# Hybrid decoder trunk: a linear recurrence in chunks of 64 tokens instead of 32

## The chip, the cores and the metric

One core of one Trainium2 chip runs the whole program. The metric is the device time of one execution in microseconds, lower is better. All matrix work is on TensorE (PE in the rows; its weight loads are PEld); VectorE (DVE), ScalarE (ACT) and GpSimd (POOL) do the elementwise work; SyncE (SP) issues the large loads.

## What is computed

Two layers on 256 tokens of width 2048. Each: a modulated RMS norm, one projection `h @ W_in`, four groups of heads side by side (A: an RWKV-7 recurrence, B: stick-breaking attention, C: dilated attention, D: differential attention), `concat @ W_out`, a residual, a second norm and a SwiGLU block. The change is in A, eight heads of width 64:

```python
def step(state, inp):
    r_t, w_t, k_t, v_t, kk_t, b_t = inp
    sa = jnp.einsum('bhvk,bhk->bhv', state, -kk_t)
    state = (state * w_t[:, :, None, :] + sa[..., None] * b_t[:, :, None, :]
             + v_t[..., None] * k_t[:, :, None, :])
    return state, jnp.einsum('bhvk,bhk->bhv', state, r_t)
...
mu = jnp.mean(y, axis=-1, keepdims=True)
y = ((y - mu) * lax.rsqrt(var + RWKV_LN_EPS)).reshape(B, S, C) * ln_w + ln_b
return (y + bonus.reshape(B, S, C)) * g
```

In layer 1, `v` is first mixed with the `v` of layer 0.

## The kernel before

The weights stream in through SyncE's queue; ScalarE and VectorE split most of them into a high and a low float32r part (tiles `hi`, `lo`), and TensorE takes three products for each (names `hh`, `hl` for the activations). The order of all instructions is written at build time by a small planner: `quad` (line 534) writes the weight products, and between them `tick` (484) lets generators ("jobs") write their next piece once their inputs should be ready by an estimated clock (`spend`, 250). Each engine then runs its instructions in that order. PSUM has four banks for jobs, handed out by `bank` (309) and `drop` (320). `rwkv` (942) runs at a higher priority than the attention jobs; `self.width` bounds how many of these run at once.

Group A goes in three stages. (1) `rw_head_pair` (828), for two heads at a time: decays, scaled keys, `kq` (removal keys and receptances), then lines 892 to 907: products of the keys with `kq` for each chunk of 32 tokens, in a bank for each head of the pair, masked by VectorE into `ab`; `bh`, `kh` and `v` are transposed into `TM`. (2) `rwkv` lines 995 to 1024: the 64 triangular 32x32 blocks are inverted by substitution on VectorE (tiles `at`, `xt`, `iv`), through DRAM (`scr`, `scr2`) into `TT`. (3) Lines 1026 to 1104: eight steps, one for each chunk. `state_part` and `chunk_part` are the products of state and of values; a step has three hand-overs (`yield`): sums for the keys, evacuated by ScalarE to `sa0`; the inverse, evacuated to `sa`; the new state, evacuated by VectorE to `S`, and the sums for the outputs, which stay in two banks `XY` for four steps. `group_norm` (1123) then normalises four chunks at a time, adds `bonus` and multiplies by `gate` (both kept in SBUF since stage 1). The projection `W_out` reads the tiles `ys` in the order B and C, A, D (`WO`, line 30) and the build waits for a tile that isn't written yet (`need`, 528).

In the rows a product in plain float32 shows as two MATMUL instructions. All lines of the trace carry L180, the helper that records each operation, so groups are told apart by their tiles: `m<-S,kq` is state by keys, `m<-tm,ab` values by key products, `m<-sa,TT` the inverse, `m<-tm` and `m<-sa,tm` the new state, `m<-sa,ab` the corrected values for the outputs, `m<-kq,a` and `m<-kq,sh` the key products of a head pair, `q<-...` weight products, `m<-qk,qk` scores, `m<-v,aT` a product of group D.

## Time and profile before

| | |
|---|---|
| median of three runs | 2662.35 us (2657.1 to 2662.5) |
| the profiled execution | 2661.86 us, span 2660.1 us, mean granted clock 0.986 |
| TensorE busy | 2594.6 us (98% of the span) |
| VectorE, ScalarE, GpSimd busy | 1802.8, 1121.6, 107.6 us |

A row of the timeline has the start in microseconds from the span's beginning, the time from the first start to the last end of the group, the engine, the tiles written and read, rows*columns of the array and the shape of the moving operand, and the count; in brackets the idle time of the engine before it and what ended it. Matmuls overlap, so the time that a group takes from TensorE is the distance between its start and that of the next row. The rows of a stretch give the busy time of each engine in it, then the granted TensorE clock (1.00 is 2.4 GHz, 0.50 is 1.2 GHz), the mean busy share of the DMA engines and GB/s.

### The profile page before, as it was taken

How to read it: one execution, taken by the hardware profiler on the slowest of the kernel's cores; microseconds unless marked ns; L12 is line 12 of the kernel's file. 1: busy time of each engine (PE TensorE's matmuls, PEld its weight loads, DVE VectorE, ACT ScalarE, POOL GpSimd, SP SyncE). 2: the span in 40 equal slices, each digit the busy share in tenths (PEclk: the TensorE clock that was granted, in tenths of full speed). 3: DMA queues.
4: the chain of work that ended last, by engine and by line, in shares of the span. 5: the costliest groups of instructions: out<-in, count | busy, mean ns of one | idle time of the engine just before them, and what ended most of it. 6: DMA issues, size and time to landing. Idle time of an engine off the chain costs nothing.

```text
span 2660.1 us, 43002 instructions
## 1 busy us (share of the span) xinstructions
PE 2594.6 (98%) x17446; PEld 2296.8 (86%) x17446; DVE 1802.8 (68%) x2922; ACT 1121.6 (42%) x1579; POOL 107.6 (4%) x208
## 2 busy tenths in 40 slices
PE   7999999999999999999999999999999999999998
PEld 4888887887898898898899998889888988988987
DVE  6667875669887787764577888677755455455555
ACT  2315543324434433433455444456444344344343
POOL 0001110000000000000020011000100000000001
PEclk9999998999999999999999999999899999999999
DMA  9895664897888898865466677576455555555553
GB/s 357 310 373 205 228 221 164 280 347 267 322 338 324 315 340 316 308 230 190 175 256 255 252 281 253 209 254 247 147 186 190 190 188 182 185 189 190 186 188 117
DMA packets 133609, 648.70 MB, mean 244 GB/s; under 512 B 17685, under 2 KB 23853, under 8 KB 86177
## 3 DMA queue, kind: packets, MB, share of 16 engines
q1 hardware_dynamic: 126306, 632.66, 65.0%
q0 software_dynamic: 6528, 12.25, 1.5%
q8 instruction: 136, 2.23, 0.3%
q10 hardware_dynamic: 576, 1.05, 0.1%
q14 instruction: 63, 0.52, 0.1%
HBM read 640.61 MB, written 7.62 MB: 244 GB/s over the span
## 4 chain that ended last, share of the span: by engine, by line
PE 90%; DVE 4%; DMA 3%; ACT 1%; issue 1%; SPq 0%; DVEq 0%; ACTq 0%
PE q L180 75%; PE m L180 14%; DMA ar<-wada 2%; DVE ar L180 1%; DVE lo L180 1%; DVE x L180 0%; PE st L180 0%; DMA raw<-wst 0%; DMA x<-xt 0%; ACT hi L180 0%; DVE rstd L180 0%; DVE out L180 0%; ACT sh L180 0%; SPq L180 0%; ACT L180 0%
## 5 line engine op out<-in xcount | busy, mean ns | idle before, releaser
L180 DVE TENSOR_TENSOR lo<-raw,hi 128x1024 fp32r<-128x1024 f32 (+1 forms) x742 | 903.1, 1225 | 531.1 <-ACT hi L180 526.1
L180 ACT ACTIVATE hi<-raw 128x1024 fp32r<-128x1024 f32 (+1 forms) x742 | 779.8, 1057 | 936.8 <-PE q L180 756.4
L180 DVE SCALAR_TENSOR_TENSOR ar<-ar,cond 128x1024 f32<-128x1024 f32 x384 | 462.6, 1219 | 42.3 <-DMA ar<-wada 41.6
L180 PE MATMUL q<-hi,hh 128*128 128x512 f32 x1456 | 457.0, 395 | 6.8 <-ACT hh L180 6.8
L180 PE MATMUL q<-lo,hh 128*128 128x512 f32 x1456 | 455.6, 394 | 0.0
L180 PE MATMUL q<-hi,hl 128*128 128x512 f32 x1456 | 451.9, 392 | 0.0
L180 PEld LDWEIGHTS q<-hi,hh 128*128 128x128 f32 x1456 | 271.7, 190 | 63.2 <-ACT hh L180 7.9
L180 PEld LDWEIGHTS q<-hi,hl 128*128 128x128 f32 x1456 | 275.0, 189 | 58.7
L180 PEld LDWEIGHTS q<-lo,hh 128*128 128x128 f32 x1456 | 272.4, 189 | 58.2 <-issue 1.7
L180 PE MATMUL q<-ah,hi 128*128 128x256 f32 x1344 | 216.6, 283 | 0.0
L180 PE MATMUL q<-ah,lo 128*128 128x256 f32 x1344 | 216.1, 283 | 0.0
L180 PE MATMUL q<-al,hi 128*128 128x256 f32 x1344 | 216.1, 283 | 0.0
L180 PEld LDWEIGHTS q<-ah,hi 128*128 128x128 f32 x1344 | 185.9, 192 | 0.6
L180 PEld LDWEIGHTS q<-al,hi 128*128 128x128 f32 x1344 | 185.5, 192 | 0.0
L180 PEld LDWEIGHTS q<-ah,lo 128*128 128x128 f32 x1344 | 185.5, 192 | 0.0
L180 PE MATMUL q<-hh,hi 128*128 128x256 f32 (+1 forms) x1040 | 179.6, 293 | 5.1 <-ACT hh L180 3.4
L180 PE MATMUL q<-hh,lo 128*128 128x256 f32 (+1 forms) x1040 | 178.7, 292 | 4.2 <-DVE lo L180 4.1
L180 PE MATMUL q<-hl,hi 128*128 128x256 f32 (+1 forms) x1040 | 172.6, 286 | 0.0
L180 PEld LDWEIGHTS q<-hh,hi 128*128 128x128 f32 (+1 forms) x1040 | 148.2, 195 | 12.4 <-issue 4.9
L180 PEld LDWEIGHTS q<-hh,lo 128*128 128x128 f32 (+1 forms) x1040 | 146.9, 195 | 10.7 <-DVE lo L180 5.3
L180 PEld LDWEIGHTS q<-hl,hi 128*128 128x128 f32 (+1 forms) x1040 | 146.2, 194 | 0.1
L180 POOL TENSOR_TENSOR sq<-sq,sq 128x256 f32<-128x256 f32 x44 | 35.1, 798 | 1684.0 <-ACT sq L180 1681.5
(243 smaller groups left out, 2496.3 us busy)
## 6 DMA issues: line engine op xcount, KB each, us to landing
raw<-wst SPq DMA_DIRECT2D x369, 1024.0 KB, 4.9
ar<-wada SPq DMA_DIRECT2D x384, 512.0 KB, 6.7
whole<-wst SPq DMA_DIRECT2D x64, 512.0 KB, 7.5
x<-xt SPq DMA_DIRECT2D x32, 128.0 KB, 4.5
bias<-bskew POOLq DMA_DIRECT2D x24, 128.0 KB, 3.6
bskew<-bscr POOLq DMA_DIRECT2D x4, 576.0 KB, 14.0
xd<-x POOLq DMA_DIRECT2D x16, 128.0 KB, 6.9
x<-xd SPq DMA_DIRECT2D x16, 128.0 KB, 3.9
```

The costliest lines, as they stand in the source:

```text
L180: return f(*a, **kw)
```

## The change

The recurrence runs in four chunks of 64 tokens. `kq` holds, for each chunk, 64 columns of removal keys and 64 of receptances, the order turned round in odd chunks. The products of values for the keys and for the outputs share one weight tile `kar` of 128 columns, so one product writes the sums for the outputs to one half of the partitions and those for the keys to the other. The state is kept block-diagonal for two heads (128x128 in `Sx`, zero elsewhere), so state by keys and by receptances is one product for a head pair. The inverse of a 64x64 triangle is put together from two 32x32 inverses (by the same substitution) and a product of both with the block below the diagonal (tiles `NT`, `XT`, `XN`, `VS`, `TQ`). The outputs of each chunk are centred on their own and one bank is held for a chunk instead of two for four chunks. `bonus`, `gate` and the first layer's `v` go to DRAM and are loaded back where they are used. The pool of 128x512 tiles has 21 slots instead of 19, and the width for group D is 2 instead of 3. The core of the diff:

```diff
-    jj, t = p[:, None] % 32, np.arange(32)[None, :]
+    jj, t = p[:, None] % 64, np.arange(64)[None, :]
...
-    put("msk", np.concatenate([-strict, incl, strict, incl], 1))
-    put("seg", np.broadcast_to((np.arange(264) % 33 != 0).astype(np.float32), (128, 264)))
+    low = p[:, None] < 64
+    put("msk", np.concatenate([-strict, incl, np.where(low, incl, strict), np.where(low, strict, incl)], 1))
+    put("seg", np.broadcast_to((np.arange(264) % 65 != 0).astype(np.float32), (128, 264)))
...
     def T2(self, dt=F32, n="d"):
-        return self.heap.tile([128, 512], dt, tag="k2", name=self.name(n), bufs=self.cfg.get("k2", 19))
+        return self.heap.tile([128, 512], dt, tag="k2", name=self.name(n), bufs=self.cfg.get("k2", 21))
 
...
         kqj = self.T2(n="kq")
-        kq4 = kqj[:].rearrange("p (c s t) -> p c s t", s=2, t=32)
-        tt(kq4[:, :, 1, :], c3(r[j][:]), e23[:, :, 1:33], ALU.mult)
+        kq3 = kqj[:]
+        kq_r, kq_a = (bass.AP(tensor=kq3.tensor, offset=kq3.offset + o, ap=[list(kq3.ap[0]), [256, 2], [st, 2], [1, 64]])
+                      for o, st in ((0, 192), (64, 64)))
+        c4 = lambda ap: ap.rearrange("p (h g) t -> p h g t", g=2)
+        tt(kq_r, c4(c3(r[j][:])), c4(e23[:, :, 1:65]), ALU.mult)
...
+        if l == 0:
+            nc.gpsimd.dma_start(self.vfirst[j], v[j][:])
         bn = self.T(n="bn")
         tt(bn[:], p3[:, 0:256], v[j][:], ALU.mult)
         self.drop()
-        R["bonus"][j] = bn
-        yield
-        dbc = dall[:, j, :, None].to_broadcast([128, 8, 32])
+        nc.gpsimd.dma_start(R["gb"][j, :, 0, :], bn[:])
+        R["bonus"][j] = True
...
         ab = yield from self.bank(2)
-        absb = self.T2(n="ab")
-        ab3 = absb[:].rearrange("p (q n) -> p q n", q=4)
-        for e in range(2):
-            es = slice(64 * e, 64 * e + 64)
-            for c in range(8):
-                g, hf = c % 4, c // 4
-                for s, m in enumerate((bt, kt)):
-                    o = hf * 128 + s * 64
-                    nc.tensor.matmul(ab[e][32 * g:32 * g + 32, o:o + 64], m[es, c * 32:c * 32 + 32],
-                                     kq4[es, c, :, :], start=True, stop=True)
-        for e in range(2):
-            tt(ab3[:, 2 * e:2 * e + 2, :], ab[e][:, 0:256].rearrange("p (q n) -> p q n", q=2),
-               C("msk")[:, None, :].to_broadcast([128, 2, 128]), ALU.mult)
+        ba, br, kar = self.T(n="ba"), self.T(n="br"), self.T2(n="kar")
+        ba4, br4, kar4 = (t[:].rearrange("p (e h n) -> p e h n", e=2, h=2) for t in (ba, br, kar))
+        for s, m in enumerate((bt, kt)):
+            for hf in range(2):
+                for g in range(2):
+                    c = 2 * hf + g
+                    ks = [(0, 0, 128)] if s or g else [(0, 64, 64), (64, 0, 64)]
+                    for o, i, n in ks:
+                        for e in range(2):
+                            es = slice(64 * e, 64 * e + 64)
+                            o1 = hf * 256 + s * 128 + o
+                            nc.tensor.matmul(ab[e][64 * g:64 * g + 64, o1:o1 + n], m[es, c * 64:c * 64 + 64],
+                                             kqj[es, c * 128 + i:c * 128 + i + n], start=True, stop=True)
+        for t4, o, n in ((ba4, 0, 64), (br4, 64, 64), (kar4, 128, 128)):
+            for e in range(2):
+                tt(t4[:, e, :, :], ab[e].rearrange("p (h n) -> p h n", h=2)[:, :, o:o + n],
+                   C("msk")[:, None, o:o + n].to_broadcast([128, 2, n]), ALU.mult)
         self.drop(2)
-        nc.gpsimd.dma_start(R["scr"][4 * j:4 * j + 4].rearrange("q p t -> p q t"), ab3[:, :, 0:32])
+        nc.gpsimd.dma_start(R["scr"][4 * j:4 * j + 4].rearrange("q p t -> p q t"),
+                            ba[:].rearrange("p (q n) -> p q n", q=4))
...
+        R["AB"][j] = (br4, kar4)
...
-            d = self.vfirst[j]
+            d = self.T(n="vf")
+            nc.gpsimd.dma_start(d[:], self.vfirst[j])
...
+        sc_ = scr[:]
+        for e in range(2):
             for i in range(2):
-                nc.gpsimd.dma_start(at[i][64 * e:64 * e + 64, :], sc3[:, 512 * i:512 * i + 512])
+                for b in range(2):
+                    nc.gpsimd.dma_start(at[i][64 * e + b:64 * e + 64:2, :],
+                                        bass.AP(tensor=sc_.tensor, offset=sc_.offset + b * 2080 + i * 1024,
+                                                ap=[[4096, 32], [64, 16], [1, 32]]))
...
-        TTt = self.T2(n="TT")
-        TT3 = TTt[:].rearrange("p (q t) -> p q t", t=32)
+        NT = self.T2(n="NT")
+        for a in range(2):
+            nc.gpsimd.dma_start(NT[64 - 64 * a:128 - 64 * a, :].rearrange("p (q t) -> p q t", t=32),
+                                scr[:, 64 * a:64 * a + 64, 32:64].rearrange("q p t -> p q t"))
+        TQ = [self.T2(n="TT") for _ in range(2)]
+        for t in TQ:
+            nc.gpsimd.memset(t[:], 0.0)
+        XT, XN, VS = self.T2(n="XT"), self.T2(n="XN"), self.T2(n="VS")
+        X3, N3, XN3, V3 = (t[:].rearrange("p (q t) -> p q t", t=32) for t in (XT, NT, XN, VS))
         s2 = scr2[:]
         for e in range(2):
-            nc.gpsimd.dma_start(TT3[e:128:2], bass.AP(tensor=s2.tensor, offset=s2.offset + e * 64 * 512,
-                                                      ap=[[32, 64], [2048, 16], [1, 32]]))
-        yield
-
...
+                                            ap=[[32, 32], [2048, 16], [1, 32]]))
+        yield
+
+        T4 = [t[:].rearrange("p (q t) -> p q t", t=64) for t in TQ]
+        nc.vector.transpose(XN[:], XT[:])
+        for i in range(2):
+            for g in range(4):
+                P = slice(32 * g, 32 * g + 32)
+                o = g % 2 * 32
+                nc.scalar.activation(T4[i][P, :, o:o + 32], X3[P, 8 * i:8 * i + 8, :], AF.Copy)
+        yield
+        vp = yield from self.bank()
+        for q in range(16):
+            for a in range(2):
+                P, N = slice(64 * a, 64 * a + 32), slice(64 * a + 32, 64 * a + 64)
+                nc.tensor.matmul(vp[N, q * 32:q * 32 + 32], N3[P, q, :], XN3[P, q, :], start=True, stop=True)
+        for a in range(2):
+            N = slice(64 * a + 32, 64 * a + 64)
+            nc.scalar.activation(VS[N, :], vp[N, :], AF.Copy)
+        self.drop()
...
+        vp = yield from self.bank()
+        for q in range(16):
+            for a in range(2):
+                P, N = slice(64 * a, 64 * a + 32), slice(64 * a + 32, 64 * a + 64)
+                nc.tensor.matmul(vp[P, q * 32:q * 32 + 32], V3[N, q, :], X3[N, q, :], start=True, stop=True)
+        v3 = vp[:].rearrange("p (q t) -> p q t", t=32)
+        for a in range(2):
+            P = slice(64 * a, 64 * a + 32)
+            for i in range(2):
+                nc.scalar.activation(T4[i][P, :, 32:64], v3[P, 8 * i:8 * i + 8, :], AF.Copy)
+        self.drop()
+        yield
...
+        Sx = self.T2(n="S")
+        nc.gpsimd.memset(Sx[:], 0.0)
+        for c in range(4):
+            g, hf = c % 2, c // 2
+            P, H = slice(64 * g, 64 * g + 64), slice(64 - 64 * g, 128 - 64 * g)
             if g == 0:
-                XY = yield from self.bank(2)
                 sa0, sa = self.T2(n="sa0"), self.T2(n="sa")
-
-            def state_part(col, which, Sx):
+                yc, mu = self.T2(n="yc"), self.small(8)
+            vc = TM[hf][P, 2, :]
+            XY = yield from self.bank()
+            for h in range(8):
+                j, e = divmod(h, 2)
+                nc.tensor.matmul(XY[:, h * 64:h * 64 + 64], AB[j][1][P, e, hf, :], vc[:, h * 64:h * 64 + 64],
+                                 start=h == 0, stop=c == 0, skip_group_check=True)
+            if c:
                 for j in range(4):
-                    for e in range(2):
-                        es = slice(64 * e, 64 * e + 64)
-                        nc.tensor.matmul(XY[e][P, col + j * 64:col + j * 64 + 64], kq[j][es, c, which, :],
-                                         Sx[es, j * 64:j * 64 + 64], start=j == 0, stop=False, skip_group_check=True)
-
-            def chunk_part(col, w, rhs, st, en):
+                    nc.tensor.matmul(XY[:, j * 128:j * 128 + 128], kq[j][:, c * 128:c * 128 + 128],
+                                     Sx[:, j * 128:j * 128 + 128], start=False, stop=True, skip_group_check=True)
+            nc.scalar.activation(sa0[H, :], XY[H, :], AF.Copy, scale=-1.0)
...
-            if c:
-                state_part(0, 0, Sx)
-            chunk_part(0, 64, TM[hf][P, 2, :], c == 0, True)
-            s3 = sa0[P, :].rearrange("p (j e v) -> p j e v", j=4, e=2)
-            for e in range(2):
-                o3 = XY[e][P, 0:256].rearrange("p (j v) -> p j v", j=4)
-                if e and self.cfg.get("sd", 0):
-                    nc.vector.tensor_scalar(s3[:, :, e, :], o3, -1.0, None, ALU.mult)
-                else:
-                    nc.scalar.activation(s3[:, :, e, :], o3, AF.Copy, scale=-1.0)
...
             p1 = yield from self.bank()
             for h in range(8):
-                nc.tensor.matmul(p1[P, h * 64:h * 64 + 64], TT3[P, 2 * h + hf, :], sa0[P, h * 64:h * 64 + 64],
-                                 start=True, stop=True)
+                nc.tensor.matmul(p1[P, h * 64:h * 64 + 64], T4[h // 4][H, 2 * (h % 4) + hf, :],
+                                 sa0[H, h * 64:h * 64 + 64], start=True, stop=True)
             nc.scalar.activation(sa[P, :], p1[P, :], AF.Copy)
             self.drop()
             yield
-            Sprev = Sx
-            if c < 7:
+            if c < 3:
                 p2 = yield from self.bank()
-                for s, m in ((1, TM[hf][P, 2, :]), (0, sa[P, :])):
+                for s, m in ((1, vc), (0, sa[P, :])):
                     for h in range(8):
                         j, e = divmod(h, 2)
                         es = slice(64 * e, 64 * e + 64)
                         nc.tensor.matmul(p2[es, j * 64:j * 64 + 64], TM[hf][P, s, h * 64:h * 64 + 64],
                                          m[:, h * 64:h * 64 + 64], start=s == 1 and j == 0, stop=s == 0,
                                          skip_group_check=True)
-                Sx = self.T(n="S")
...
+                for e in range(2):
+                    es = slice(64 * e, 64 * e + 64)
+                    d3 = Sx[es, :].rearrange("p (j v) -> p j v", j=4)[:, :, 64 * e:64 * e + 64]
+                    p3 = p2[es, 0:256].rearrange("p (j v) -> p j v", j=4)
+                    if Sd is None:
+                        nc.vector.tensor_copy(d3, p3)
+                    else:
+                        tt(d3, p3, Sd[es, :].rearrange("p (j v) -> p j v", j=4), ALU.add)
...
-            if c:
-                state_part(256, 1, Sprev)
-            chunk_part(256, 96, TM[hf][P, 2, :], c == 0, False)
-            chunk_part(256, 32, sa[P, :], False, True)
-            if g == 3:
-
-                mu, var = self.small(8), self.small(8)
...
-                self.add(self.group_norm(l, hf, yc, sq, var, R), 1)
+            for h in range(8):
+                j, e = divmod(h, 2)
+                nc.tensor.matmul(XY[P, h * 64:h * 64 + 64], AB[j][0][P, e, hf, :], sa[P, h * 64:h * 64 + 64],
+                                 start=False, stop=True, skip_group_check=True)
+            yield
...
+            y3 = XY[P, :].rearrange("p (h v) -> p h v", h=8)
+            nc.vector.tensor_reduce(mu[P, :], y3, mybir.AxisListType.X, ALU.add)
+            nc.vector.tensor_scalar(mu[P, :], mu[P, :], -1.0 / 64, None, ALU.mult)
+            tt(yc[P, :].rearrange("p (h v) -> p h v", h=8), y3, mu[P, :, None].to_broadcast([64, 8, 64]), ALU.add)
+            self.drop()
+            if g == 1:
+                self.add(self.group_norm(l, hf, yc, self.T2(n="ysq"), self.small(8), R), 1)
...
-            R["gate", j] = g
+            nc.gpsimd.dma_start(R["gb"][j, :, 1, :], g[:])
+            R["gate", j] = True
...
+        gb = []
+        for j in range(4):
+            t = self.T(n="gb")[:].rearrange("p (w n) -> p w n", w=2)
+            nc.gpsimd.dma_start(t, R["gb"][j, :, :, hs])
+            gb.append(t)
...
             yo = R["yo"][j]
-            nc.vector.tensor_tensor(yo[:, hs], yo[:, hs], R["bonus"][j][:, hs], ALU.add)
-            nc.vector.tensor_tensor(yo[:, hs], yo[:, hs], R["gate", j][:, hs], ALU.mult)
+            nc.vector.tensor_tensor(yo[:, hs], yo[:, hs], gb[j][:, 0, :], ALU.add)
+            nc.vector.tensor_tensor(yo[:, hs], yo[:, hs], gb[j][:, 1, :], ALU.mult)
...
-                    self.width = self.cfg.get("dw", 3)
+                    self.width = self.cfg.get("dw", 2)
```

## Rows read from the trace of the kernel before

**Rows 1.** The page: totals of TensorE, and the chain that ended last by engine.
```profile
PE 2594.6 (98%) x17446; PEld 2296.8 (86%) x17446; DVE 1802.8 (68%) x2922; ACT 1121.6 (42%) x1579; POOL 107.6 (4%) x208
PE 90%; DVE 4%; DMA 3%; ACT 1%; issue 1%; SPq 0%; DVEq 0%; ACTq 0%
```

**Rows 2.** Stretches: busy time (instructions) of each engine, clock, DMA share, GB/s.
```profile
378.20:494.70 116.50, 114.74 (x1292) 96.19 (x1292) 59.63 (x157) 40.38 (x92) 4.32 (x8) 0.91 0.59 198
1490.00:1625.00 135.00, 133.97 (x1198) 123.99 (x1196) 120.91 (x234) 60.54 (x89) 16.54 (x37) 1.00 0.74 264
1625.00:1747.50 122.50, 122.10 (x1441) 106.63 (x1440) 79.70 (x160) 54.50 (x103) 7.93 (x20) 0.96 0.62 217
```

**Rows 3.** Timeline of TensorE through one step of the recurrence in layer 0.
```profile
443.97 1.07 PE L180 MATMUL m<-tm,ab 32*32 32x64 f32 x16
444.98 0.73 PE L180 MATMUL q<-lo,hh 128*128 128x512 f32 x2
...
449.65 1.08 PE L180 MATMUL m<-sa,TT 32*32 32x64 f32 x16
...
452.92 0.68 PE L180 MATMUL m<-tm 32*64 32x64 f32 x16 [0.61 <-ACT aT L180]
453.43 0.64 PE L180 MATMUL m<-sa,tm 32*64 32x64 f32 x16
454.00 0.64 PE L180 MATMUL m<-S,kq 64*32 64x64 f32 x16
454.56 1.08 PE L180 MATMUL m<-tm,ab 32*32 32x64 f32 x16
455.48 1.05 PE L180 MATMUL m<-sa,ab 32*32 32x64 f32 x16
456.46 0.55 PE L180 MATMUL m<-consts,e 128*128 128x128 f32 x3
```

**Rows 4.** Timeline of TensorE: key products of a head pair, 64 instructions in all.
```profile
293.89 0.34 PE L180 MATMUL m<-kq,a 64*32 64x64 f32 x8
...
294.96 0.87 PE L180 MATMUL m<-aT,v 128*64 128x256 f32 x8
```

**Rows 5.** Timeline of TensorE: products of 128x128 with 128 moving columns.
```profile
525.60 1.50 PE L180 MATMUL m<-v,aT 128*128 128x128 f32 x12
526.94 0.60 PE L180 MATMUL q<-yo,whole 128*128 128x256 f32 x2
```

**Rows 6.** Groups by shape: weight loads of 128 and 32 columns (busy us, mean ns).
```profile
L180 PEld LDWEIGHTS m<-v,aT 128*128 128x128 f32 x48 | 6.2, 192 | 0.2
L180 PEld LDWEIGHTS m<-sa,TT 32*32 32x32 f32 x256 | 14.6, 105 | 3.9 <-issue 1.0 <-ACT sa L180 0.6 <-ACT aT L180 0.4
```

**Rows 7.** Timeline of TensorE: scores of two heads of group D.
```profile
1810.07 1.58 PE L180 MATMUL m<-qk,qk 64*128 64x128 f32 x16
```

**Rows 8.** Stretches at the lower clock: first, last and sum of six.
```profile
376.20:383.10 6.90, 4.87 (x30) 4.70 (x31) 6.71 (x27) 1.69 (x3) 0.56 (x1) 0.51 0.91 330
...
1734.80:1738.20 3.40, 3.40 (x17) 3.40 (x18) 0.27 (x1) 1.44 (x2) 0.00 (x0) 0.50 0.47 159
sum 34.20, PE 31.57 PEld 27.96 DVE 26.95 ACT 12.26 POOL 0.56; mean PE 5.26 PEld 4.66 DVE 4.49 ACT 2.04 POOL 0.09
```

**Rows 9.** Timeline where TensorE waits before the recurrence of layer 0; VectorE then.
```profile
378.23 1.91 PE L180 MATMUL m<-tm,ab 32*32 32x64 f32 x16 [5.54 <-DVE m L180]
...
375.25 1.23 DVE L180 SCALAR_TENSOR_TENSOR ar<-ar,cond 128x1024 f32<-128x1024 f32 x1 [2.95 <-DMA ar<-wada]
```

**Rows 10.** A 128x128 operation of VectorE (groups by shape); a GpSimd DMA's landing.
```profile
L180 DVE TENSOR_TENSOR yo<-yo,gate 128x128 f32<-128x128 f32 x16 | 4.7, 292 | 0.6
...
at<-scr POOLq DMA_DIRECT2D x8, 128.0 KB, 7.7
```

**Rows 11.** Timelines: VectorE gates the last output of layer 0; TensorE reads the first.
```profile
514.57 0.29 DVE L180 TENSOR_TENSOR yo<-yo,gate 128x128 f32<-128x128 f32 x1
...
517.03 1.89 PE L180 MATMUL q<-yo,whole 128*128 128x256 f32 x8
```

75 lines of the change are left out of this document (29 added, 46 removed).

## The prediction

> **What bounds the kernel now.** I read the totals and the chain first [rows 1]: TensorE is busy 2594.6 of 2660.1 us, and 90% of the chain that ended last is TensorE's. Next the stretches of busy time by stage [rows 2]. The recurrence of layer 0 lies between 378.2 and 494.7 us, that of layer 1 between 1625 and 1747.5. In both TensorE is busy nearly all the time (114.7 of 116.5, 122.1 of 122.5), the other engines are not (VectorE 59.6 and 79.7, ScalarE 40.4 and 54.5), and the DMA engines are at 0.59 and 0.62. So a microsecond of TensorE's work taken out there should be a microsecond of the span. In the stage before, where the heads are prepared and the 32x32 inverses are made (1490 to 1625), VectorE is at 120.9 of 135: work added to it there is nearly on the path.
>
> Then TensorE in order of time through one step of the recurrence [rows 3]. What counts is not the duration of a matmul (they overlap) but the distance from a group's start to the next one's. Each float32 product is two instructions, so a group of 8 products shows as x16. Values for the keys take 1.01 us (443.97 to 444.98). The inverse, of the same shape and busy as long (1.08 against 1.07): 1.00. New state: 0.51 and 0.57. State for the outputs 0.56, and state for the keys the same. Values for the outputs 0.92, the corrected values for the outputs 0.98. In all 6.11 us a step.
>
> **The change part by part.**
> *Before, per layer.* Eight steps are 48.9 us; the first has no state (two groups, 1.12 us less), the last makes none (1.08 less): 46.7. The products of keys with keys in each head pair [rows 4]: 64 instructions from 293.89 to 294.96, 1.07 us, four times: 4.3. Sum 51.0.
>
> *After, per layer*, at 2.4 GHz:
> - Values for keys and outputs in one product: 8 products with 128 weight columns and 64 moving columns, 4 times. No row has this shape. With 64 moving columns and few weights an instruction comes every 62 ns (1.00 us for 16 [rows 3]); with 128 weight and 128 moving columns every 112 ns (12 in 1.34 us [rows 5]). Loading 128 columns lasts 192 ns, 32 columns 105 ns [rows 6], so each column adds 0.9 ns and 128 of them need about as long as those 112 ns: I take a value near the upper row, 106 ns, 1.7 us a group, 6.8 us; ends 4.0 and 7.2.
> - Block-diagonal state: 4 products of 128x128 with 128 moving columns, three times: 24 instructions of 112 ns [rows 5], 2.7.
> - Inverse: 8 products with 64 moving columns on one half of the rows, four times: 1.00 each [rows 3], 4.0.
> - New state: 16 products in two column halves, three times: 0.51 + 0.57 [rows 3] = 1.08 each, 3.2; if the halves did not overlap, 6.0.
> - Corrected values for the outputs: 0.98 [rows 3], four times, 3.9.
> - Composing the inverse: 64 products of 32x32, 128 instructions. Tiles all over the array come every 17 ns (1.07 us over 64 [rows 4]), two alternating ones every 35 ns (0.56 over 16 [rows 3]): 2.2 to 4.5, I take 2.6, near the lower as these move half as many columns.
> - Keys with keys: per head pair 24 instructions of 128 moving columns and 16 of 64, two row halves alternating. The short ones at 35 ns are 0.56 us. The long ones at twice that are 1.68; no row has them, the scores (64x128, columns 128 and 256 mixed) come every 99 ns at most (1.58 over 16 [rows 7]), and at twice 17 ns they would be 0.82. I take 2.2 us a pair, 8.8 a layer; ends 4.4 and 11.8.
>
> Sum 6.8 + 2.7 + 4.0 + 3.2 + 3.9 + 2.6 + 8.8 = 32.0 us, so 19.0 us less per layer, 38.0 in both. With all lower ends 24.4 and with all upper ends 40.1: 21.8 to 53.2 us in both layers. This is the term that carries the forecast.
>
> *Switches.* Each burst of small products costs some 0.09 us more at its edge (the values group takes 1.01 before a weight product and 0.92 before another small one [rows 3]). 24 bursts a layer become 14: 1.8 us less in both.
>
> *The clock.* Six stretches in and just before the two recurrences run at 1.2 GHz (granted clock 0.50 to 0.51), 34.2 us in all [rows 8]. A stretch at half rate costs half its length, 17.1 us. Five of them begin in or right after a burst of small products, such as that ending at 1734.8; the first follows the idle 5.54 us at 378.23 [rows 9]. The longest burst now is new state through outputs, 3.54 us [rows 3]; after, it is values plus state, 2.6 us. I expect half of these stretches to go, 8 us; ends 0 and 17.
>
> *The wait at the recurrence's start.* TensorE stands 5.54 us at 378.23 for VectorE, which itself stands 2.95 us for a modulation weight's DMA [rows 9]. The change moves this moment but not its cause: 0, ends -5.5 and +5.5.
>
> *VectorE.* Two masks of 128x256 per head pair become two such and four of 128x128 (0.29 us each by [rows 10]): 4.6 us a layer, in the stage where it is 90% busy [rows 2]. Centring the outputs goes from four parts of 256 columns to four of 512, and a transpose of 128x512 comes; the halved count of state updates pays some of that back. These lie in the recurrence, where it has 40 us free. I put +4 us on the path for the masks of both layers; ends 0 and 12.
>
> *What I cost at nothing, and its cover.* ScalarE: sixteen copies of 32x256 and eight of 32x512 become eight of 64x512 and fourteen copies for the composition; it is 35 to 45% busy there [rows 2]. GpSimd's queue gets some 28 more DMAs a layer (bonus, gate and first values out and in, the blocks of the inverse in 128-byte pieces). Behind a store that waits for ScalarE or VectorE stand the bias loads of the softmax groups, the selects of the stick-breaking heads and the partial sums of squares; those run well ahead of their readers, as no row of TensorE names GpSimd beside the recurrence. Without that cover a late DMA costs its landing, 7.7 us [rows 10]. The four differential heads at width two go in two rounds as at three (three and one): 0, ends ±6.
>
> *The chain of the recurrence itself.* Today it has little to spare in layer 0: its last gated output starts at 514.57 and the projection reads the first at 517.03 [rows 11]. After, that reader comes some 23 us earlier, at 494. Eight steps took 116.5 us with three hand-overs each, 4.9 us a hand-over. Now there are three more for composing and four steps of four: 19 x 4.9 = 93 us instead of 116.5. The group norm also waits for a load, 7.7 us as above. So the outputs are ready at 514.9 - 23 + 8 = 500, up to 6 us late; but hand-overs are shorter where TensorE's bursts are. I count 0; ends 0 and +8.
>
> Sum, against the profiled execution's own 2661.9 us (span 2660.1, the rest lies around it; the median of the runs is 2662.35, so the same within 0.02%): 2661.9 - 38.0 - 1.8 - 8 + 4 = 2618.1. **Forecast 2618 us.**
>
> *A rule that speaks against the change.* By the rows, weights are loaded behind products of the same rows: a group with 32 rows alone comes every 62 ns although each of its weight loads lasts 105 [rows 3, 6]. The Trainium skill ("TensorE: Matmul & The Clock Gate", Part 3, The mechanism) says that weight loads overlap with matmuls in flight only where the row group differs. This trace speaks against it at 32 weight columns; no row shows 128 columns on 64 rows. The same page (Part 1, "Wait — 56ns, not 53.3ns?") gives a floor of about 25 ns from start to start; the 17 ns of [rows 4] differ, and with 25 ns the composing would be 3.2 us a layer instead of 2.6.
>
> **The rivals.**
> 1. *The wide weights are not hidden.* Then the values group pays 112 + 62 = 174 ns an instruction, 2.8 us instead of 1.7, eight times: +8.8, 2627 us. For it: the shape is new. Against: the 62 ns of [rows 3]. It is what the Trainium skill's rule above would give.
> 2. *The upper ends meet.* Halves that don't overlap, wide key products at 99 ns, clock stretches that stay, the chain late by 8: 2661.9 - 21.8 + 4 = 2644 without, 2652 with the late chain. For it: several shapes without a row.
> 3. *Slower: the clock.* If the products of 64 rows and 64 columns leave TensorE at 1.2 GHz through both recurrences, as after some of today's bursts, some 95 us in each (116.5 less 21) cost half again what they hold: the 34 us that are slow already count, so (190 - 34) / 2 = +78 against -40: 2700. It decides from 80 us of additional slow time. Against it: at 2.6 us the longest burst is shorter than now and weight products lie between.
> 4. *It does not do what it says for TensorE's time*: fewer and larger products but the same columns moved, so 2662 within 5. Only if the array overlapped 32x32 tiles in the chain as it does in the key products; rows 3 show that it does not (62 ns against 17).
>
> **How the numbers follow.** Forecast with its own ends (2600 to 2626) 0.55; more gain (2585 to 2600, clock and lower ends together) 0.12; rival 1 0.10; rival 2 0.13; rival 4 0.04; rival 3 0.06. The range that leaves out no more than 2 in 10: 2596 to 2648. A measurement of this kernel tells about 0.2% (5 us) from no change. Faster 0.55 + 0.12 + 0.10 + 0.13 = 0.90, less 0.02 for mishaps of several kinds: 0.88; within 0.2% 0.05; slower 0.07.
>
> **What would show it.** In the profile after: groups of x16 values products at 1.7 us start to start (1.0 would be a further 5 us gained, 2.8 rival 1); new state at 1.1 a step; key products near 2.2 us a pair; granted clock above 0.95 through both recurrences (rival 3: near 0.5); no idle of TensorE before the gated outputs. A wait of TensorE on the outputs of the recurrence, or VectorE named before weight products in the stage of the masks for more than 10 us, would make the forecast wrong.

## The result, and the profile after

The changed kernel takes 2633.15 us (median of 4 runs, 2624.29 to 2639.07), the kernel before beside it 2662.43 (2657.1 to 2666.18): a ratio of 0.9889, 95% interval 0.9855 to 0.9922, or 29 us less. The forecast was 44 less. The profiled execution of the changed kernel is the slowest of its four, 2639.07 us (span 2637.2), so a comparison of the two traces shows 22.9 us of the 29.

The page, totals and chain of the changed kernel (against [rows 1]; the helper that records is at L181 in this kernel and at L184 in some variants):

```profile
PE 2547.7 (97%) x16214; PEld 2253.9 (85%) x16214; DVE 1816.7 (69%) x2950; ACT 1126.3 (43%) x1578; POOL 149.9 (6%) x270
PE 81%; DMA 9%; DVE 7%; ACT 1%; issue 1%; SPq 1%; POOL 0%; DVEq 0%; ACTq 0%; POOLq 0%
```

TensorE is busy 46.9 us less, but the span fell by half of that only, and TensorE's share of the chain fell from 90% to 81%: transfers (9%, from 3%) and VectorE (7%, from 4%) took its place. The two recurrences, with the stage before the second between them (stretches as in [rows 2]: busy time of PE, PEld, DVE, ACT, POOL, then clock, DMA share, GB/s):

```profile
424.30:491.90 67.60, 65.33 (x530) 54.04 (x529) 49.58 (x140) 23.12 (x61) 5.30 (x8) 1.00 0.86 292
1483.00:1666.20 183.20, 179.03 (x1486) 160.74 (x1485) 153.68 (x287) 91.75 (x139) 37.78 (x75) 0.99 0.77 259
1666.20:1733.00 66.80, 66.28 (x654) 60.37 (x654) 56.90 (x145) 34.09 (x69) 5.06 (x9) 1.00 0.72 257
```

A recurrence takes 67 us where it took 116 to 122, at full clock. But it also starts late: at 424.3 instead of 378.2 in layer 0, at 1666 instead of 1625 in layer 1. One step of it on TensorE (timeline; what a group takes is the distance to the next row's start, as in [rows 3]):

```profile
442.10 2.00 PE L181 MATMUL m<-tm,kar 64*128 64x64 f32 x16
444.02 1.16 PE L181 MATMUL m<-S,kq 128*128 128x128 f32 x8
444.94 0.70 PE L181 MATMUL q<-hi,hh 128*128 128x512 f32 x2
...
448.55 1.14 PE L181 MATMUL m<-sa,TT 64*64 64x64 f32 x16
449.62 0.55 PE L181 MATMUL m<-consts,e 128*128 128x128 f32 x3
...
451.83 0.68 PE L181 MATMUL m<-tm 64*64 64x64 f32 x16
452.34 0.63 PE L181 MATMUL m<-sa,tm 64*64 64x64 f32 x16
452.81 1.09 PE L181 MATMUL m<-sa,br 64*64 64x64 f32 x16
453.84 0.87 PE L181 MATMUL m<-aT,v 128*64 128x256 f32 x8
```

Values 1.92 us, state 0.92, inverse 1.07, new state 0.98, corrected values 1.03: 5.9 us for 64 tokens, where 32 took 6.1. And the products of keys with keys of one head pair, 1.10 us for 40 instructions (against [rows 4]):

```profile
312.94 0.73 PE L181 MATMUL m<-kq,a 64*64 64x64 f32 x24
313.46 0.65 PE L181 MATMUL m<-kq,sh 64*64 64x128 f32 x16
314.04 0.70 PE L181 MATMUL m<-sh,consts 128*128 128x256 f32 x2
```

**Where the time went.** TensorE makes 14,048 products with the projections' weights in both kernels, in the same order. I cut both traces at the same n-th of them, so that each stretch holds the same weight products (microseconds; idle: gaps of TensorE over 0.25 us; low clock: time granted 1.2 GHz; rest: everything else TensorE did, from start to start):

```
stretch                               before   after  differ.   idle         low clock    rest
start, first projections               178.7   183.1   +4.4    14.6 19.3     6.8  3.4     0.0  0.0
layer 0, head pairs                    100.4   104.7   +4.3     2.7  6.2     3.4 10.2    27.5 27.3
layer 0, inverse to output projection  275.8   260.5  -15.3     7.7 16.8    23.9 20.5    76.2 56.4
layer 0, feed-forward                  738.2   737.8   -0.4     5.0  4.5     6.8  6.8    10.1 10.1
layer 1, first projections             115.6   116.4   +0.8     3.4  3.4     3.4  6.8     2.7  2.7
layer 1, head pairs to recurrence      338.3   314.3  -24.0     1.3  4.6    10.2  3.4    92.3 68.9
layer 1, rest of output projection     115.9   122.9   +7.0     2.3  6.3     0.0  3.4     9.0  9.9
layer 1, feed-forward                  759.5   759.5    0.0     6.4  6.5    13.7 13.7    12.4 12.4
```

The jobs lie differently against these cuts (the head pairs of the changed kernel end in the third stretch), so the lines are read together with their neighbours. TensorE's idle gaps grew from 43.4 to 67.6 us in all, 24.2 more, so half of the 46.9 us that it is less busy came back as waiting. It lies in the stretch with layer 0's recurrence (third line), in the start (first, before the changed part), in the head pairs (second) and in layer 1 (sixth and seventh). The two waits behind layer 0's recurrence, on the timelines of TensorE, and of VectorE with one row of ScalarE:

```profile
497.28 1.70 PE L181 MATMUL m<-qk,qk 64*128 64x128 f32 x16
503.35 0.96 PE L181 MATMUL m<-consts,yc 128*128 128x128 f32 x4 [4.37 <-DVE yc L181]
509.78 0.47 PE L181 MATMUL m<-consts,e 128*128 128x128 f32 x1 [5.47 <-DVE e L181]
...
513.27 3.62 PE L181 MATMUL q<-yo,whole 128*128 128x256 f32 x8
```

```profile
502.60 0.69 DVE L181 TENSOR_TENSOR yc<-yc,s 128x512 f32<-128x512 f32 x1
...
504.34 1.51 ACT L181 ACTIVATE yo<-m,vecs 128x128 f32<-128x128 f32 x4 [0.73 <-PE m L181]
504.70 1.22 DVE L181 SCALAR_TENSOR_TENSOR ar<-ar,cond 128x1024 f32<-128x1024 f32 x1
...
510.42 2.19 DVE L181 TENSOR_TENSOR yo<-yo,gb 128x128 f32<-128x128 f32 x8
```

TensorE has run out of other work at 499 and stands 4.37 and 5.47 us; the recurrence's outputs are gated from 510.42 on and read at 513.27. The first wait is for the recurrence's group norm (`yc`); the second names `e`, the softmax of group D. ScalarE had written the outputs by 505.85, but in VectorE's order three modulation steps of 1.22 us and this softmax stand before their gating, so the last 4.6 us are VectorE's order and not the recurrence. In the kernel before, the last output was ready 2.2 us ahead of the first one's reader (514.57 + 0.29 to 517.03 [rows 11]). And the clock falls there:

```profile
503.50:517.20 13.70, 7.34 (x24) 5.42 (x24) 13.06 (x44) 6.06 (x21) 0.00 (x0) 0.50 0.42 140
```

### The profile page after: what moved, and what is told of

Same layout as the page of the kernel before. It is cut to its first block, busy times and chain, and to the rows that moved or that the text cites. A ratio compares the mean times of both kernels' runs of the same rounds, so it can differ in the third digit from the quotient of the medians.

```text
span 2637.2 us, 40726 instructions
## 1 busy us (share of the span) xinstructions
PE 2547.7 (97%) x16214; PEld 2253.9 (85%) x16214; DVE 1816.7 (69%) x2950; ACT 1126.3 (43%) x1578; POOL 149.9 (6%) x270
## 4 chain that ended last, share of the span: by engine, by line
PE 81%; DMA 9%; DVE 7%; ACT 1%; issue 1%; SPq 1%; POOL 0%; DVEq 0%; ACTq 0%; POOLq 0%
PE q L181 70%; PE m L181 10%; DMA ar<-wada 4%; DMA raw<-wst 3%; DVE ar L181 2%; DVE lo L181 1%; DMA gb<-gate 1%; DVE x L181 1%; SPq L181 1%; DMA x<-xt 1%; ACT hi L181 1%; DMA x<-xd 0%; PE st L181 0%; DVE iv L181 0%; DMA up<-ups 0%
## 5 line engine op out<-in xcount | busy, mean ns | idle before, releaser
L181 DVE TENSOR_TENSOR lo<-raw,hi 128x1024 fp32r<-128x1024 f32 (+1 forms) x742 | 904.2, 1226 | 530.0 <-ACT hi L181 529.0
L181 ACT ACTIVATE hi<-raw 128x1024 fp32r<-128x1024 f32 (+1 forms) x742 | 781.5, 1058 | 966.8 <-PE q L181 773.4
L181 DVE SCALAR_TENSOR_TENSOR ar<-ar,cond 128x1024 f32<-128x1024 f32 x384 | 463.7, 1220 | 69.6 <-DMA ar<-wada 68.8
L181 PE MATMUL q<-hi,hh 128*128 128x512 f32 x1456 | 456.3, 395 | 6.9 <-ACT hh L181 6.8
L181 PE MATMUL q<-lo,hh 128*128 128x512 f32 x1456 | 454.1, 393 | 0.0
L181 PE MATMUL q<-hi,hl 128*128 128x512 f32 x1456 | 451.1, 391 | 0.0
L181 PEld LDWEIGHTS q<-hi,hl 128*128 128x128 f32 x1456 | 274.6, 189 | 58.8 <-issue 0.2
L181 PEld LDWEIGHTS q<-hi,hh 128*128 128x128 f32 x1456 | 270.6, 189 | 62.7 <-ACT hh L181 8.0
L181 PEld LDWEIGHTS q<-lo,hh 128*128 128x128 f32 x1456 | 272.3, 189 | 57.5 <-issue 1.7
L181 PE MATMUL q<-ah,hi 128*128 128x256 f32 x1344 | 216.5, 283 | 0.0
L181 PE MATMUL q<-ah,lo 128*128 128x256 f32 x1344 | 216.1, 283 | 0.0
L181 PE MATMUL q<-al,hi 128*128 128x256 f32 x1344 | 216.0, 283 | 0.0
L181 PEld LDWEIGHTS q<-ah,hi 128*128 128x128 f32 x1344 | 185.9, 192 | 0.6
L181 PEld LDWEIGHTS q<-al,hi 128*128 128x128 f32 x1344 | 185.5, 192 | 0.0
L181 PEld LDWEIGHTS q<-ah,lo 128*128 128x128 f32 x1344 | 185.5, 192 | 0.0
L181 PE MATMUL q<-hh,hi 128*128 128x256 f32 (+1 forms) x1040 | 177.3, 290 | 5.9 <-ACT hh L181 3.4
L181 PE MATMUL q<-hh,lo 128*128 128x256 f32 (+1 forms) x1040 | 177.7, 290 | 2.8 <-DVE lo L181 2.7
L181 PE MATMUL q<-hl,hi 128*128 128x256 f32 (+1 forms) x1040 | 172.1, 285 | 0.0
L181 PEld LDWEIGHTS q<-hh,hi 128*128 128x128 f32 (+1 forms) x1040 | 146.5, 194 | 12.9 <-issue 4.7
L181 PEld LDWEIGHTS q<-hh,lo 128*128 128x128 f32 (+1 forms) x1040 | 146.2, 194 | 9.5 <-issue 4.5
L181 PEld LDWEIGHTS q<-hl,hi 128*128 128x128 f32 (+1 forms) x1040 | 145.9, 193 | 0.0
L181 POOL TENSOR_TENSOR sq<-sq,sq 128x256 f32<-128x256 f32 x44 | 35.1, 799 | 1717.0 <-ACT sq L181 1714.5
## 6 DMA issues: line engine op xcount, KB each, us to landing
bskew<-bscr POOLq DMA_DIRECT2D x4, 576.0 KB, 20.5
```

The costliest lines, as they stand in the source:

```text
L181: return f(*a, **kw)
```

## The experiments

A ratio is to the kernel before, measured beside it on the same chip. The changed kernel's own four runs spread over 14.8 us, and the interval of its ratio (0.9855 to 0.9922) overlaps with those of all its variants below but number 7 and number 11. So a gain of 7 to 12 us over it, taken between medians, is hardly clear of noise by itself; the stretches of the traces, one execution each, say where it lies.

**1. Is it the 128 weight columns that make the values product slow?** Each is made as two products into the two column halves:

```diff
-   nc.tensor.matmul(XY[:, h * 64:h * 64 + 64], AB[j][1][P, e, hf, :], vc[:, h * 64:h * 64 + 64],
-                    start=h == 0, stop=c == 0, skip_group_check=True)
+   for Z in (P, H):
+       nc.tensor.matmul(XY[Z, h * 64:h * 64 + 64], AB[j][1][P, e, hf, Z], vc[:, h * 64:h * 64 + 64],
+                        start=h == 0, stop=c == 0, skip_group_check=True)
```

> The changed kernel, but each values product with 128 weight columns is made as two products of 64 weight columns, one into each half of the output's rows; nothing else is altered. In the changed kernel an instruction of this group starts every 120 ns (1.92 us a group of 16, eight groups in both layers). Theory: with 128 columns the load of the weights is what the 120 ns are made of, and it is not fully hidden; products in alternating column halves overlap as those of the new state do (some 30 ns each), so that a group of 32 instructions takes 0.9 to 1.1 us, TensorE saves 6 to 8 us, and the time falls by 3 to 8 us (less than TensorE's saving, if the first layer's end is set by the chain of the recurrence). Rival: the weight columns of a whole group are loaded one after the other however they are divided, so that 32 instructions come every 60 to 66 ns, the group takes 1.9 to 2.1 us as now, and the time stays within 3 us of the changed kernel's 2633.

Measured: 2626.54 us, ratio 0.985 (0.983 to 0.987). Groups by shape, the changed kernel and then this one (busy us, mean ns):

```profile
L181 PE MATMUL m<-tm,kar 64*128 64x64 f32 x128 | 16.0, 275 | 0.0
L181 PEld LDWEIGHTS m<-tm,kar 64*128 64x128 f32 x128 | 14.9, 188 | 1.9 <-issue 1.2 <-PE q L181 0.4
```

```profile
L181 PE MATMUL m<-tm,kar 64*64 64x64 f32 x256 | 9.2, 221 | 0.0
L181 PEld LDWEIGHTS m<-tm,kar 64*64 64x64 f32 x256 | 8.1, 135 | 2.1 <-issue 1.4 <-DVE s L181 0.3
```

```profile
443.99 1.15 PE L181 MATMUL m<-tm,kar 64*64 64x64 f32 x32
445.07 1.16 PE L181 MATMUL m<-S,kq 128*128 128x128 f32 x8
```

A group of twice as many instructions takes 1.08 us instead of 1.92: 34 ns an instruction instead of 120. The theory holds: the 120 ns are the wide weights, not the 64 moving columns, and two column halves hide each other's loads. The split changes two things at once, the width and the taking in turn; rows of the changed kernel above tell them apart. The corrected values, 64 weight columns always in the same half, come every 64 ns (1.03 us over 16), the new state, whose column halves are taken in turn, every 31 (0.98 over 32). TensorE saves 6.8 us; the medians differ by 6.6, within the spread of the changed kernel's runs.

**2. What does the late recurrence of layer 0 cost?** Nobody waits for it:

```diff
+   of = lambda k: k + 4 if l == 0 and k < 4 else k
...
-   self.need(lambda: kt in self.ys)
+   self.need(lambda: of(kt) in self.ys)
...
-   if k not in yp and k in self.ys:
-       y = self.ys[k]
+   if k not in yp and of(k) in self.ys:
+       y = self.ys[of(k)]
```

> The changed kernel, but in layer 0 the output projection reads the four outputs of the stick-breaking heads where it reads the four of the recurrence; the recurrence is computed as before, and nobody waits for it in that layer (so the result of that layer is another one). This prices the lateness of the recurrence's outputs. Theory: after the change the recurrence of layer 0 ends too late for its reader; the idle 4.37 and 5.47 us of TensorE at 503 and 510 us and half of the 13.65 us at the low clock around them go, 10 to 17 us in all: 2616 to 2623 us. Rival: what came back is TensorE's or VectorE's work, or a clock that stays low without the idle time; then the idle moves elsewhere and the time is within 5 us of 2633.

Measured: 2622.89 us, 0.9824 (0.9793 to 0.9856). The stretch from the inverse to the output projection of layer 0 takes 247.7 us instead of 260.5, idle 8.1 instead of 16.8, low clock 6.8 instead of 20.5. So the lateness is worth 10 to 13 us.

**3. Is it the planner, which holds a job until its store should have landed?**

```diff
+   def store(self, dst, src):
+       ready = self.cur.ready
+       self.nc.gpsimd.dma_start(dst, src)
+       self.cur.ready = ready
-   nc.gpsimd.dma_start(R["gb"][j, :, 0, :], bn[:])
+   self.store(R["gb"][j, :, 0, :], bn[:])
```
(and so for gate, first values and `scr`.)

> The changed kernel, but the planner no longer holds a job back for the estimated end of a store that nobody in that job reads (bonus, gate, first values, and the products of the keys on their way to the inverse); the stores themselves and every real wait stay. Theory: those stores hold the head pairs of layer 0: the step after the bonus starts 17 us after it in the first pair (271.7 after 254.4 us), 4.7 us in the kernel before. Then here the step follows within 8 us, the first values product of layer 0 starts at 390 to 410 us instead of 424, the idle before the gated outputs is under 3 us, and the time is 2615 to 2626. Rival: the chain is late because of its true transfers and hand-overs (inverse, composition): the first values product starts after 418 and the time is within 5 us of 2633.

Measured: 2630.52 us, 0.9868 (0.9847 to 0.9889): the rival's size. The loads for the inverse start at 323.4 instead of 337.1, as the theory wanted, but the first values product at 425.0, not earlier than 424.3. Two places where the 13 us went, as I read the rows of VectorE and ScalarE of this run (no run changes either alone):

```profile
267.25 0.41 DVE L181 TENSOR_TENSOR bh<-a,dall 128x256 f32<-128x256 f32 x1
277.70 0.43 DVE L181 TENSOR_TENSOR bh<-a,dall 128x256 f32<-128x256 f32 x1 [8.25 <-PE m L181]
```

```profile
406.35 1.06 ACT L181 ACTIVATE hi<-raw 128x1024 fp32r<-128x1024 f32 x1 [11.20 <-DMA raw<-wst]
407.31 0.83 ACT L181 ACTIVATE TT<-XT 32x256 f32<-32x256 f32 x2
```

The first pair's step after the bonus now follows at once, the second pair's only after 8.25 us; and the composition's copies stand in ScalarE's order behind a conversion that waits 11.20 us for its weights. Composing takes from 409.0 to 420.2 (first to second product) instead of 416.5 to 420.0. The planner's holding alone is not what makes the recurrence late.

**4. The detour through memory alone, in the kernel before** (its three stores and their loads, 21 wide buffers, chunks of 32):

```diff
-   R["bonus"][j] = bn
+   nc.gpsimd.dma_start(R["gb"][j, :, 0, :], bn[:])
-   R["gate", j] = g
+   nc.gpsimd.dma_start(R["gb"][j, :, 1, :], g[:])
+   nc.gpsimd.dma_start(self.vfirst[j], v[j][:])
...
```

> The kernel before (chunks of 32), with one part of the change alone: bonus, gate and the first layer's values go through memory as in the changed kernel, with 21 wide buffers instead of 19. Theory: this part alone delays the recurrence of layer 0 by 15 to 30 us, whose outputs had 2.5 us to spare; TensorE stands before the gated outputs, and the time is 2670 to 2690 us against 2662. Rival: the stores ride beside other work; the time is within 5 us of 2662, and the lateness in the changed kernel comes from its new arithmetic (masks, composition).

Measured: 2687.46 us, 1.0076 (1.0046 to 1.0106): 22.7 us slower. Its trace, TensorE at the end of layer 0's recurrence:

```profile
536.19 1.09 PE L180 MATMUL m<-consts,yc 128*128 128x128 f32 x4 [1.91 <-DVE yc L180]
540.41 4.95 PE L180 MATMUL q<-yo,whole 128*128 128x256 f32 x11 [3.14 <-DVE yo L180]
```

The first values product is at 396.9 instead of 378.2, the reader at 540.4 instead of 517.0. I had expected all of it in layer 0, but cut as above layer 0's third stretch is 18.4 us longer, and the two of layer 1 are 9.5 and 3.8 longer. Part of it is the clock: 88.7 us of this trace up to 2600 us are at 1.2 GHz, 68.3 in the kernel before.

**5 and 6. Reading the outputs later** (in layer 0 the first two quarters of the output projection take group A in their last pass), in the changed kernel and in the kernel before:

```diff
    for i, part in enumerate(WO[:2]):
-       put("w_out", l, g, part, whole=i in PLAIN[l])
-put("w_out", l, outs, WO[2], whole=2 in PLAIN[l])
+       if i == 0 or l or g[0][0] == "o2":
+           put("w_out", l, g, part, whole=i in PLAIN[l])
+if l == 0:
+    put("w_out", l, outs[:2], WO[1] + WO[2], whole=2 in PLAIN[l])
+put("w_out", l, outs[2 if l == 0 else 0:], WO[2], whole=2 in PLAIN[l])
...
```

> The changed kernel; in layer 0 the first two quarters of the output projection take the recurrence's outputs in their last pass, beside those of the differential heads, and not in their first (the same products, in another order; the last two quarters as before). So the first reader of these outputs comes about 27 us later. Theory: the recurrence's end in layer 0 costs 10 us because it comes after its reader, as the run in which nobody waited for it showed (2622.9 against 2633.2); here 2618 to 2626, with no idle of TensorE before the gated outputs and no low clock between 495 and 525 us. Rival: the gain of that run came from the work or the transfers it avoided, not from the wait; then the wait moves to another group's outputs and the time is 2629 to 2637.

> The kernel before, with the same later reading of the recurrence's outputs in layer 0 and nothing else. Theory: in that kernel these outputs were ready 2.5 us before they were read, so there is no wait to remove: 2657 to 2668 against 2663. Rival: the order of the projection is better in itself (weights' transfers, VectorE's load at that point), whatever the recurrence does: under 2655.

Measured: 2621.61 us, 0.9844 (0.9823 to 0.9866), in the changed kernel; 2662.46, 0.9997 (0.9988 to 1.0007), in the kernel before. The reader in the changed kernel's variant, with nothing before it that waits:

```profile
531.79 1.89 PE L184 MATMUL q<-yo,whole 128*128 128x256 f32 x8
```

The same edit gains 11.5 us between medians where the outputs were late and nothing where they were not. This is the wait's price, with the whole computation done; the stretch falls from 260.5 to 246.3, and its low clock from 20.5 to 3.4, while the head pairs' stretch before it is 4.1 longer (108.8), with a stall of 7.85 us before the gates' products.

**7. Later reading and split together** (the edits of numbers 1 and 5).

> The changed kernel with both: the recurrence's outputs of layer 0 read in the last pass, and each values product of 128 weight columns made as two of 64. Theory: the two are separate costs (10 us of waiting in layer 0; 7.5 us of TensorE's work in two layers), so they add up: 2633 - 10 - 7 = 2616, 2611 to 2620. Rival: the split saved mostly by bringing the late outputs forward (in layer 0 its saving and the wait are the same microseconds), and the sum is 2621 to 2626.

Measured: 2615.84 us (2611.7 to 2625.06), 0.9829 (0.9808 to 0.985). The median is the theory's; the interval holds the rival too. In the stretch itself the two add up: 260.5 falls by 5.6 with the split, by 14.2 with the later reader, by 19.5 with both. But the head pairs' stretch grew to 108.3 (104.7), with a longer stall before the gates' products, and took 3.6 of it back. It has the lowest median of the versions run, 47 us below the kernel before and some 17 below the changed one.

**8. Width two of the differential heads, in the kernel before** (`self.cfg.get("dw", 3)` to 2):

> The kernel before, with the differential heads at width two as in the changed kernel and nothing else. Theory: two rounds of heads instead of three and one make the last heads' outputs later by some us, and TensorE stands for them at the end of the projection in layer 1 (1.49 and 1.01 us in the changed kernel): 2662 to 2668 against 2663. Rival: width two spreads VectorE's and ScalarE's work so that it costs nothing or gains: 2655 to 2662.

Measured: 2663.14 us, 1.0008 (0.9992 to 1.0024): no difference, as I had put it in the sum.

**9. The stores on another queue** (the three stores of the changed kernel):

```diff
-   nc.gpsimd.dma_start(R["gb"][j, :, 0, :], bn[:])
+   nc.scalar.dma_start(R["gb"][j, :, 0, :], bn[:])
...
```

> The changed kernel; the stores of bonus, gate and first values are issued by ScalarE's queue instead of GpSimd's, nothing else (the planned order is the same). Theory: on GpSimd's queue these stores stand behind the four copies of the bias table (22 us from issue to landing in layer 0), so their buffers come free late: VectorE's first step after the bonus waits 3.0 us for the store of a gate at 271.7 us (up to 9.8 in the later runs), its masks come late, and TensorE stands 3.5 us (up to 8.9) for them. Then here this idle time of TensorE at 274 us is under 1 us, the recurrence of layer 0 comes 3 to 8 us earlier, and the time is 2623 to 2630 against 2633. Rival: the wait is for the buffer in any case (too few of them), or ScalarE, which now waits for VectorE's bonus before its own work, loses as much: within 3 us of 2633.

Measured: 2639.65 us, 0.9898 (0.9871 to 0.9926), the changed kernel's own ratio. The theory falls; the stall of the gates' products is still there, on TensorE's timeline of this run:

```profile
277.67 4.90 PE L181 MATMUL m<-sh,up 32*128 32x256 f32 x10 [5.24 <-DVE kar L181]
```

**10 and 11. Numbers 1, 3 and 5 together,** with the stores on GpSimd's and on ScalarE's queue:

> The changed kernel with three edits: the recurrence's outputs of layer 0 read in the last pass, values products split in two column halves, and stores not awaited by the planner. Theory: in layer 1 the stores' holding alone costs 8.6 us (428.6 us from the first input weights to the end of the projection when they were not awaited, 437.2 in the changed kernel), because the recurrence ends some 26 us earlier and the differential heads start earlier; in layer 0 it is masked by the other lateness. So against 2615.8 of the run with the two other edits: 2605 to 2611. Rival: with stores in flight and not awaited, buffers come free later and the stall before the gate's products (8.9 us) grows: 2613 to 2620.

> The changed kernel with four edits: outputs of layer 0 read in the last pass, values products split, stores not awaited, and these stores (with that of the products of the keys) issued by ScalarE's queue. Theory: the costs are separate, and without the stall before the gate's products (up to 8.9 us in layer 0) the time is 2598 to 2607. Rival: ScalarE's queue, which then waits for VectorE's results, holds back the conversion of weights: the time is not below that of the run with three edits, 2608 to 2620.

Measured: 2621.73 us, 0.9829 (0.9796 to 0.9862), and 2617.23 us, 0.9822 (0.9792 to 0.9853). Neither is below number 7; by the ratio all three are level. The end of layer 1's projection did become shorter (115.4 and 116.4 us; 122.9 in the changed kernel), and the stall before the gates' products went; the third stretch became longer by 6.7 and 9.1 than in number 7, with twice its idle time. Both theories fall; number 11 has the time of its rival, whose reason no row here shows.

**12. The detour undone in the changed kernel:** bonus, gate and first values stay on chip, the arithmetic of 64 tokens untouched.

```diff
-   nc.gpsimd.dma_start(R["gb"][j, :, 0, :], bn[:])
-   R["bonus"][j] = True
+   R["bonus"][j] = bn
...
```

> The changed kernel with one part undone: bonus, gate and the first layer's values stay on chip as in the kernel before (64 buffers of 256 columns and 20 of 512 instead of 62 and 21); the arithmetic of the chunks of 64 is untouched. Theory: alone in the kernel before, this detour cost 22 us, by making the recurrence of layer 0 late for its reader; so without it the head pairs of layer 0 end about 10 us earlier, the first values product starts before 415 us (424 in the changed kernel), the wait before the gated outputs shrinks from 9.8 to under 4 us, and the time is 2612 to 2626. Rival: as in the run whose stores were not awaited, the earlier recurrence meets other waits (transfers of weights, composition's copies, its three more hand-overs), so that only its place moves: within 5 us of 2633.

Measured: 2623.09 us (2618.78 to 2624.48), 0.9843 (0.9821 to 0.9866). The first values product starts at 414.9, and TensorE hardly waits (its timeline):

```profile
501.91 0.73 PE L181 MATMUL m<-consts,on 128*128 128x128 f32 x2 [2.10 <-DVE on L181]
505.44 12.04 PE L181 MATMUL q<-yo,whole 128*128 128x256 f32 x48
```

So the detour costs some 10 us in the changed kernel. By stretches, layer 0's third is 7.3 us shorter than with it, and the rest of layer 1's projection 9.4 (113.5 against 122.9); some of that comes back elsewhere (layer 0's head pairs +1.8, layer 1's recurrence +2.1). In that part of layer 1 the changed kernel waits for the last heads of group D, which have no such row here; its timeline of TensorE:

```profile
1844.36 0.74 PE L181 MATMUL q<-yh,hi 128*128 128x256 f32 x4 [1.49 <-ACT yh L181]
1847.29 0.74 PE L181 MATMUL q<-yh,hi 128*128 128x256 f32 x4 [1.01 <-ACT yh L181]
```

Numbers 2, 5 and 12 remove most of the wait in three ways, by another operand, a later reader and an earlier writer, and give 2622.9, 2621.6 and 2623.1. That the three agree so closely is luck in part: number 12 gains as much in layer 1 as in layer 0. Without the detour, with the later reader and the split was not run.

## Why the prediction was right, and where it was off

The sign and the mechanism held: small products taken out of TensorE's recurrence shorten the span, since TensorE is the bound there. The size held to two thirds, 29 us of 44: 2633 lies in the range (2596 to 2648), but outside the forecast's own ends (2600 to 2626), and a sign that I had named against the forecast came, a wait of TensorE on the recurrence's outputs. The step "a microsecond of TensorE's work taken out there should be a microsecond of the span" held for half: 46.9 us less busy, 22.9 us less span. That the time is no further off is luck for a part: TensorE's products saved more than forecast, and that made up for a clock that gave nothing.

*TensorE's products.* From start to start, over both layers (the small differences to the rows above are edges):

```
                                       forecast  measured
values for keys and outputs              13.6      15.4
block-diagonal state                      5.4       5.7
inverse                                   8.0       8.6
new state                                 6.4       5.9
corrected values for the outputs          7.8       8.3
composing the inverse                     5.2       4.5
keys with keys                           17.6       8.8
sum after                                64.0      57.1
sum before                              102.0     105.9
```

So 48.8 us less, where I had 38.0 and 1.8 for the switches. In the kernel before, 8.3 of the 105.9 us ran at 1.2 GHz, none after, so some 4 of the 48.8 are clock. Six of seven terms are within 14%. The mis-sized one is keys with keys: I took 70 ns for the products with 128 moving columns, from the scores [rows 7]; in alternating row halves they come every 36 ns (16 in 0.58 us), and 24 instructions that mix 64 and 128 columns every 22 (0.52 us). The lower end that I gave, twice the 17 ns of [rows 4], was the nearer row.

*Rival 1* fell: an instruction of the values group takes 120 ns, near the 106 of the forecast and not 174. But its object was real, as experiment 1 shows. The Trainium skill's rule ("TensorE: Matmul & The Clock Gate", Part 3, The mechanism), that weight loads overlap only where the row group differs, does not agree with these rows: in the split both halves lie on the same 64 rows, a load takes 135 ns, and an instruction starts every 34.

*The clock* term did not come: -8 forecast, nothing measured in the sum. Up to 2600 us, 68.3 us are at the lower clock in both kernels. The stretches of before lay around the bursts of small products [rows 8] and those are gone (1.00 in both recurrences, so rival 3 fell with them); all but one of the new ones came where TensorE had just stood idle, the longest, 13.7 us, from the end of the wait at 503 on and over the one at 510. With the later reader the low clock in that stretch falls from 20.5 to 3.4 us, with later reader and split to 6.8. The sum over the whole trace differs more between variants than such a term is worth (41.0 and 64.9 us in these two).

*The wait at the recurrence's start* (0, ends -5.5 and +5.5) is gone: nothing waits before the first values product at 424.3. Two stalls of 2.61 and 1.17 us at 352 and 354, for a copy by ScalarE, take back 3.8 of the 5.5.

*The chain of the recurrence* was the step that failed. I wrote "up to 6 us late" and counted 0, ends 0 and +8; it is 11.5 by experiment 5. My estimate of 19 hand-overs at 4.9 us gave outputs at 500 and was short by 10 to 13 us (gated from 510.42 to 512.61). The recurrence lasts 48.9 us less, but starts 46.1 later, where I had counted 15 for composing. The group norm's load, which I had at 7.7 us, added nothing: from the last product of the recurrence to the last gated output are 20.7 us, 20.1 before. So the outputs are ready only 2.3 us earlier, while their reader, its waits taken off, comes some 14 earlier. Of the 46.1 us, 32.0 lie before the loads for the inverse, which GpSimd issues (kernel before, changed kernel, and number 12):

```profile
305.15 1.10 POOL L180 DMA_DIRECT2D at<-scr  x2 [0.93 <-PE q L180]
...
337.06 5.12 POOL L181 DMA_DIRECT2D at<-scr  x8 [0.25 <-issue]
...
316.96 3.35 POOL L181 DMA_DIRECT2D at<-scr  x5 [0.38 <-PE q L181]
```

The head pairs finish later: the step after the bonus comes 17.3 us after it in the first pair (271.66 after 254.39), 4.7 in the kernel before. I had costed the new stores at nothing because "no row of TensorE names GpSimd beside the recurrence". That is true of TensorE; the stores act on the jobs and buffers of the chain that feeds it, as VectorE's timeline of the changed kernel shows:

```profile
254.39 0.42 DVE L181 TENSOR_TENSOR bn<-m,sh 128x256 f32<-128x256 f32 x1
...
271.66 0.43 DVE L181 TENSOR_TENSOR bh<-a,dall 128x256 f32<-128x256 f32 x1 [3.03 <-DMA gb<-gate]
```

But the stores are the smaller part of the late start. Without the detour (number 12) the loads start 20.1 us earlier, and the first values product, at 414.9, only 9.4: 36.7 of the 46.1 us stay, with the rest of the change. No run takes these apart, so what they are made of stays open.

*The masks* had +4 us; the head pairs' stretch of layer 0 is 4.3 longer, of which 3.50 is one stall of TensorE for the last mask (its timeline, changed kernel):

```profile
274.08 4.13 PE L181 MATMUL m<-sh,up 32*128 32x256 f32 x10 [3.50 <-DVE kar L181]
```

It is not the masks alone: without the detour this stall is gone, and the stretch is no shorter (106.5). What sets its length stays open.

*Width two* cost nothing that a run could tell, as in the sum. The end of the projection in layer 1 (+7.0) had no term; experiment 12 puts it to the detour, and number 3, where that part takes 112.7 us with the stores in place, to the planner's holding for them.

Together: -48.8 for the products, +11.5 for the wait in layer 0, +7.0 at the end of layer 1's projection, +4.3 in the head pairs: -26.0. The traces differ by -22.9. These terms overlap and leave some out; the strict account is the one above, 46.9 us less busy and 24.2 us more idle (9.1 in layer 0's third stretch, 4.7 in the start, 4.0 at the end of layer 1's projection, 3.5 in the head pairs of layer 0, 3.3 from layer 1's head pairs through its recurrence, -0.4 elsewhere). Of rival 2's parts only the late chain and the clock that gave nothing came; its upper ends for TensorE did not. The time lies between the two, 15 us above the forecast and 11 below the rival's 2644. The start is 4.4 us longer, in weights' conversions before the changed part; it was 179.7 to 185.9 in all traces with the new arithmetic and 178.7 to 181.3 in the four without. Why was not settled.

## What to carry to other kernels

Take the products out where TensorE is the bound, but then follow the chain that feeds the reader from its first job: the reader comes earlier by what was saved, and a chain with 2 us to spare is late at once. Moving a tile to memory to free a buffer is not free because nobody on the critical engine reads it; price it at the job that issues the store, and at the engine that next needs the buffer. When a reader can be moved instead of a writer made faster, try that first: some 11 us came from the order of four weight blocks.
